# The adaLN half rows of the projection stages are loaded through GpSimd's queue instead of SyncE's, in a hybrid decoder layer on one core

## Chip, core and metric

One NeuronCore of one Trainium2 chip runs the kernel. The metric is the device time of one execution in microseconds (us); the median of three runs before the change is 1996.33 (1995.65 to 1997.18).

The engines are TensorE (PE in the profile, with PEld for its weight loads), VectorE (DVE), ScalarE (ACT), GpSimd (POOL) and SyncE (SP). Each has its own instruction stream, which it works off in order. A transfer between device memory (HBM) and the on-chip memory (SBUF) is issued by an instruction on the stream of one engine, here SP or POOL, and is then moved by the core's 16 DMA engines. An instruction that must wait for a buffer holds up all that stands behind it on its stream, so the stream of SP or POOL is spoken of as a queue.

## What is computed

One decoder layer in float32, for one sequence of 512 tokens and width 2048. A conditioning vector c gives six modulation vectors of 2048 (adaLN):

```
mod = (silu(c) @ w_ada + b_ada).reshape(B, 6, D)        # sh1, sc1, gt1, sh2, sc2, gt2
h = rmsnorm(x, g_mix) * (1 + sc1) + sh1
q, k, v, xr, xg = split(h @ w_in)                       # 5 x 1024 columns
o_attn = stick_breaking_attention(q, k, v)              # 8 heads of 128
xr = causal_depthwise_conv(xr)                          # 4 taps
o_lru = rg_lru(xr) * gelu(xg)
mixed = concat(rmsnorm(o_attn), rmsnorm(o_lru))
x = x + gt1 * (mixed @ w_out)
h = rmsnorm(x, g_mlp) * (1 + sc2) + sh2
x = x + gt2 * (relu(h @ w_mlp_in) ** 2 @ w_mlp_out)
out = rmsnorm(x, g_final)
```

## The kernel before, in words

**Matmuls.** A float32 operand is split into a rounded high part and a low part, and a product is three passes of TensorE (`mm3`, L258 to L263): high x high (L259), weight high x activation low (L262), weight low x activation high (L263). A weight tile comes from HBM into a raw buffer `wr` (`weights`, L236, on SP), ACT copies its high part (L244), VectorE subtracts to get the low part (L245, shown as L122, the helper that records it). There are four `wr` buffers and three each of the high and low parts `wh` and `wl`.

**Modulation rows.** The modulations are not computed on TensorE. Each block of 128 outputs of one modulation is a row block of the transposed `w_ada`: 128 partitions x 2048 values, worked off as two half rows of 128 x 1024 (512 KB). VectorE multiplies each half row by silu(c) (the two tiles `cb`) and sums it in the same instruction (L211); a small step adds the two sums and the bias into `mods` (L220). Six modulations of 16 blocks make 192 half rows. `Rows` (L186 to L222) handles five of the six: `rows` holds SC1 and SH1 (64 half rows, tags EARLY, used from the start of the program to about 195 us), `rows2` holds GT1, SC2 and SH2, in this order (96 half rows). `Rows.load(n, tags)` takes a buffer and issues the next n loads; `Rows.row` makes a modulation's block out of two half rows and loads what is missing. In before all of them are issued on SP.

Until the last X gate group the half rows of `rows2` go with MID: they take buffers "x" only, of which there are four, and are loaded when they are needed, two at a time. From L770 on they go with LATE: buffers "x" and "tt" in turn, five loaded ahead (L771), one more after each half row used.

**Order of the work.** The program is written as a main line of matmul groups with background lanes, generators of small pieces. At each `tick` of the main line a lane may be given pieces, at the lane's pace. A scheduler then places all instructions of each engine by priority; `later()` keeps an instruction at the place at which it was written, relative to the others so marked. Up to about 195 us: the front (norm, conv columns), the first Q and K group. Then `qk_group(2)`, `v_group(4)`, `qk_group(4)`, `qk_group(6)`, `xg_group(0)`, `xg_group(4)`, and the output projection with `w_out` (`product`, L838 to L853), up to about 650 us, with `ensure(GT1)` (L843) ahead of its first evacuation and `ensure(SC2)`, `ensure(SH2)` (L849, L850) near its end. The MLP, some 1340 us, follows.

The lanes beside these groups:

- `pair(h)`: attention of two heads. Scores on TensorE, a causal mask (L635), exponentials on ACT (L637 to L639), sums on VectorE (L641), ACT again (L644), a low part (L645, shown as L122), then cumulative sums as matmuls (L654), and shares (L663 to L666).
- `lru_shift` (L519 to L546): sums the 16 row blocks of the conv columns of `w_in`, each weighted by SH1 (L537), into `accb`. `accb` and the loaded blocks are buffers "x"; `accb` is kept until the 16 matmuls of L542 have read it. Then conv (L551 to L556), gates (L563 to L567, in "x" buffers) and scans (L580).
- `adas(GT1)`, `adas(SC2)`, `adas(SH2)`: the half rows of `rows2`, put into the lane `bg2` ahead of `v_group(4)`.

Evacuations of the groups: Q and K with ACT and VectorE (L459, L460), V with L483 and L484, the output projection with L831 and L362. POOL does two all-reduces over partitions in this part of the program (L336, in the norms of the two mixer halves), and stores the new x to HBM (L1033).

Of the kernel before, what the change touches and what calls it, by code (L numbers as in the profile page):

```python
# [64 lines left out]
def hybrid_layer_kernel(  # L65
# [13 lines left out]
    nc = tc.nc  # L79
# [18 lines left out]
    def T(tag, dt=F32, cols=None):  # L98
        return new(next(split_tag) if tag == "w4" else tag, dt, cols)
# [79 lines left out]
    def later(ins):  # L179
        return tc.keep_in_program_order(ins)  # L180
# [5 lines left out]
    class Rows:  # L186
# [4 lines left out]
            self.tiles = {}  # L191

        def load(self, n, tags):
            queue = nc.sync if tags is MID else nc.sync if tags is LATE else nc.sync
            for _ in range(n):
                if self.todo and tags:
                    i, q = self.todo.pop(0)
                    t = T(next(tags))[:, :1024]
                    later(queue.dma_start(t, w_adaT[i * P : (i + 1) * P, q * 1024 : (q + 1) * 1024]))
                    self.tiles[i, q] = t  # L200
# [24 lines left out]
    MID = itertools.cycle(["x"])  # L225
    LATE = itertools.cycle(["x", "tt"])
# [42 lines left out]
    class Lane:  # L269
# [8 lines left out]
        def next(self):  # L278
            if not self.queue:
                return False  # L280
            try:
                self.wait += next(self.queue[0]) or 0.0
            except StopIteration:
                self.queue.pop(0)
            return True
# [19 lines left out]
    def ending(load, step, ks, done, dt=0.5):  # L305

        w = [load(k) for k in ks]
        for o in range(4):
            for k, w_ in zip(ks, w):
                step(k, w_, [o])  # L310
            done(o)
            tick(dt)
# [94 lines left out]
    EARLY = itertools.cycle(["x", "tt"] * 3 + ["x"])  # L407
# [97 lines left out]
    def v_group(h0):  # L505
        bs = [bank("mm") for _ in range(4)]
        load, step = lambda k: weights(src_v(k, h0, 4)), lambda k, w, os: v_mm(bs, w, k, os)
        for k in range(NK - 2):
            step(k, load(k), range(4))
            tick()  # L510
        ending(load, step, range(NK - 2, NK), lambda o: v_evac(bs, h0, [o]))
# [848 lines left out]
    tags = ["w4"] * 3 + ["w3"] * 2 + ["w4"] * 2 + ["w3"]  # L1360
# [108 lines left out]
```

## Time and profile before

| | before |
|---|---|
| median of 3 runs | 1996.33 us (1995.65 to 1997.18) |
| profiled execution | 1994.49 us, its span 1992.7 |
| granted TensorE clock | 0.996 of full speed, over the whole span |
| busy: TensorE, VectorE, ScalarE, GpSimd | 97%, 88%, 54%, 10% |
| DMA, mean over the span | 223 GB/s; in 230 to 345 us 174, in 520 to 650 us 290 |
| loads of half rows by SP, whole run | 108 into "x" (median landing 5.6 us), 52 into "tt" (6.2 us) |

The span is what the profiler recorded from the first to the last instruction; the execution's own time is 1.8 us longer. The page's busy shares are averages over stages with different limits, so the table of busy time by stretch is read beside them. In the lists of waits a line says which engine stood idle ahead of which instruction, and what ended the wait, as total, number and longest, in us. In a timeline a row is: start, duration, engine, line, operation, what it writes and reads, and in brackets the idle time before it and what ended it. "DMA to landing" is the time from issue to arrival.

### The profile page before, as it was taken

What the parts mean: (1) busy time and instruction counts of PE and PEld (TensorE: products, weight loads), DVE (VectorE), ACT (ScalarE), POOL (GpSimd) and SP (SyncE); (2) the same over time, 40 slices, a digit from 0 to 9 for tenths busy, and PEclk for the clock granted to TensorE, in tenths of its full rate; (3) what the DMA queues carried; (4) which work ended last, traced back from release to release, by engine and by line L of the source; (5) the groups of instructions that cost most, each with busy time, mean ns of one, the idle gap of its engine ahead of it and who ended that gap; (6) DMA issues with size and microseconds to landing.
All of it is one profiled execution on the core that took longest, in us unless ns stands there. A gap on an engine that the chain in (4) does not pass through costs nothing. (4 is left out here: it accounts for less than half of the span.)

```text
span 1992.7 us, 37203 instructions
## 1 busy us (share of the span) xinstructions
PE 1941.9 (97%) x14148; PEld 1815.3 (91%) x14148; DVE 1760.6 (88%) x2979; ACT 1074.6 (54%) x1580; POOL 193.6 (10%) x307
## 2 busy tenths in 40 slices
PE   8999999999999998999999999999999999999997
PEld 6787887788888998999999999999999999999996
DVE  8998776988998599999999999999879779879996
ACT  5443564786433385555555555556445555556552
POOL 0000000000000000112111211200110210211100
PEclk9999999999999999999999999999999999999998
DMA  9896655556779544766666665755567668679653
GB/s 368 304 340 198 212 163 185 179 163 218 226 251 365 170 134 129 239 194 213 221 196 203 226 197 190 232 173 210 185 241 262 238 249 278 220 253 341 225 197 112
DMA packets 205238, 443.51 MB, mean 223 GB/s; under 512 B 20481, under 2 KB 42113, under 8 KB 205058
## 3 DMA queue, kind: packets, MB, share of 16 engines
q1 hardware_dynamic: 176338, 356.58, 54.2%
q0 software_dynamic: 23680, 77.61, 10.5%
q10 hardware_dynamic: 5040, 6.93, 1.0%
q8 instruction: 111, 1.82, 0.4%
q14 instruction: 69, 0.57, 0.1%
HBM read 376.30 MB, written 64.75 MB: 221 GB/s over the span
## 5 line engine op out<-in xcount | busy, mean ns | idle before, releaser
L1102 PE MATMUL ps_mm<-a,w 128*128 128x256 f32 x1696 | 469.1, 277 | 3.0 <-DVE a L1114 1.2
L1104 PE MATMUL ps_mm<-a,w 128*128 128x256 f32 x1696 | 469.2, 277 | 0.4 <-DVE w L122 0.3
L1103 PE MATMUL ps_mm<-a,w 128*128 128x256 f32 x1696 | 469.1, 277 | 0.4 <-DVE a L122 0.3
L1072 ACT ACTIVATE w<-ts 128x1024 fp32r<-128x1024 f32 x244 | 258.4, 1059 | 273.1 <-DVE ts L1068 241.5
L1104 PE MATMUL ps_z<-a,w 128*128 128x256 f32 x1304 | 362.0, 278 | 6.9 <-DVE w L122 6.8
L1102 PE MATMUL ps_z<-a,w 128*128 128x256 f32 x1304 | 362.2, 278 | 3.4 <-DVE a L1118 1.6
L1103 PE MATMUL ps_z<-a,w 128*128 128x256 f32 x1304 | 361.4, 277 | 0.1
L122 DVE TENSOR_TENSOR w<-ts,w 128x1024 fp32r<-128x1024 f32 x244 | 297.8, 1221 | 55.4 <-PE ps_mm L1103 20.4
L1102 PEld LDWEIGHTS ps_mm<-a,w 128*128 128x128 f32 x1696 | 318.4, 188 | 4.3 <-issue 2.5
L1104 PEld LDWEIGHTS ps_mm<-a,w 128*128 128x128 f32 x1696 | 318.7, 188 | 1.1 <-DVE w L122 1.0
L1103 PEld LDWEIGHTS ps_mm<-a,w 128*128 128x128 f32 x1696 | 318.7, 188 | 0.8 <-DVE a L122 0.8
L122 DVE TENSOR_TENSOR w<-raw,w 128x768 fp32r<-128x768 f32 (+1 forms) x296 | 267.5, 905 | 37.8 <-ACT w L244 24.0
L1066 ACT ACTIVATE w<-raw 128x768 fp32r<-128x768 f32 x244 | 204.5, 839 | 174.8 <-issue 80.5
L1104 PEld LDWEIGHTS ps_z<-a,w 128*128 128x128 f32 x1304 | 245.6, 189 | 8.2 <-DVE w L122 8.1
L1102 PEld LDWEIGHTS ps_z<-a,w 128*128 128x128 f32 x1304 | 245.8, 188 | 4.9 <-issue 2.1
L1103 PEld LDWEIGHTS ps_z<-a,w 128*128 128x128 f32 x1304 | 245.7, 188 | 0.6 <-DVE a L122 0.6
L244 ACT ACTIVATE wh<-wr 128x512 fp32r<-128x512 f32 (+1 forms) x184 | 113.2, 618 | 142.4 <-PE ps_mm L262 61.8
L1060 DVE TENSOR_TENSOR ts<-raw 128x512 f32<-128x512 f32 x244 | 166.8, 684 | 14.2 <-DMA raw<-in_w_mlp_out_dram 13.4
L259 PE MATMUL ps_mm<-a,wh 128*128 128x512 f32 x448 | 176.8, 395 | 2.6 <-DVE a L460 1.0
L263 PE MATMUL ps_mm<-a,wl 128*128 128x512 f32 x448 | 175.0, 391 | 1.5 <-DVE wl L122 1.3
L262 PE MATMUL ps_mm<-a,wh 128*128 128x512 f32 x448 | 174.9, 390 | 0.0
L211 DVE SCALAR_TENSOR_TENSOR x<-x,cb 128x1024 f32<-128x1024 f32 x108 | 131.2, 1218 | 23.4 <-DMA x<-in_w_adaT_dram 23.3
(336 smaller groups left out, 4007.7 us busy)
## 6 DMA issues: line engine op xcount, KB each, us to landing
raw<-in_w_mlp_out_dram SPq DMA_DIRECT2D x124, 512.0 KB, 4.6
raw<-in_w_mlp_in_dram SPq DMA_DIRECT2D x120, 512.0 KB, 3.8
x<-in_w_adaT_dram SPq DMA_DIRECT2D x108, 512.0 KB, 5.6
wr<-in_w_in_dram SPq DMA_DIRECT2D x160, 256.0 KB, 3.4
tt<-in_w_adaT_dram SPq DMA_DIRECT2D x52, 512.0 KB, 6.2
part<-a POOLq DMA_DIRECT2D x84, 256.0 KB, 3.9
a<-part SPq DMA_DIRECT2D x84, 256.0 KB, 6.3
prod<-a POOLq DMA_DIRECT2D x63, 256.0 KB, 5.8
```

Of the source, the lines that this page charges most:

```text
L122: tt(out=out, in0=full, in1=f32(high), op=ALU.subtract)
L211: ins = stt(out=t, in0=t, scalar=1.0, in1=cb[q_], op0=ALU.mult, op1=ALU.mult, accum_out=self.ga[:, q_ : q_ + 1],)
L244: act(h[:, :n], r[:, :n], AF.Copy)
L259: first = mm(out, wh, ah, start=start, stop=False, **kw)
L262: mm(out, wh, al, start=False, stop=False, **kw)
L263: mm(out, wl, ah, start=False, stop=stop, **kw)
L1060: tt(out=t[:, : 2 * HT].rearrange("p (a b) -> p a b", a=2), in0=r[:, HT : 3 * HT].rearrange("p (a b) -> p a b", a=2), in1=r[:, q_(0)].unsq ...
L1066: act(h, r[:, HT:], AF.Copy)
L1072: act(h, t, AF.Copy)
L1102: mm(out, wh[:, blk(i)], ah, start=st, stop=False, **kw)
L1103: mm(out, wh[:, blk(i)], al, start=False, stop=False, **kw)
L1104: mm(out, wl[:, blk(i)], ah, start=False, stop=j == js[-1], **kw)
```

## The change

Of the half rows, those of `rows` stay on SP; the 96 of `rows2` are issued by GpSimd:

```
-            queue = nc.sync if tags is MID else nc.sync if tags is LATE else nc.sync
+            queue = nc.sync if tags is EARLY else nc.gpsimd
```

Buffers, tags and arithmetic stay as they are. The number of instructions on TensorE, VectorE and ACT is the same; SP has 96 rows fewer, POOL 96 more. The scheduler places the loads anew, and with them VectorE's multiplications.

SP's queue at about 225 to 250 us, the weights of `qk_group(2)` and `v_group(4)` (wr) and the first half rows of GT1 (x_2448, x_2450, x_2521); - is before alone:

```order
 L236 DMA wr_2319<-in_w_in_dram 128x2x256
 L236 DMA wr_2393<-in_w_in_dram 128x512
-L199 DMA x_2448<-in_w_adaT_dram 128x1024
-L199 DMA x_2450<-in_w_adaT_dram 128x1024
 L236 DMA wr_2455<-in_w_in_dram 128x512
 L236 DMA wr_2477<-in_w_in_dram 128x512
 L236 DMA wr_2498<-in_w_in_dram 128x512
-L199 DMA x_2521<-in_w_adaT_dram 128x1024
```

The half rows are gone from between the weights; they stand on POOL's queue, with nothing else between them there.

VectorE at about 240 to 248 us: wl_2316, wl_2322 and wl_2396 are low parts of weights, tt_2241 a low part of attention scores, ga holds a block's two sums; + is after alone, and the rows with x are half rows of GT1:

```order
 L122 TENSOR_TENSOR tt_2241<-tt_2236,tt_2240 128x1280
 L122 TENSOR_TENSOR wl_2316<-wr_2313,wh_2315 128x512
+L220 SCALAR_TENSOR_TENSOR mods<-ga_2722,vec 128x1
+L211 SCALAR_TENSOR_TENSOR x_2813,ga_2812<-x_2813,cb_81 128x1024
+L211 SCALAR_TENSOR_TENSOR x_2815,ga_2812<-x_2815,cb_82 128x1024
+L122 TENSOR_TENSOR wl_2322<-wr_2319,wh_2321 128x512
 L545 COPY shb<-ps_z_2280 128x16
-L122 TENSOR_TENSOR wl_2322<-wr_2319,wh_2321 128x512
+L220 SCALAR_TENSOR_TENSOR mods<-ga_2812,vec 128x1
+L211 SCALAR_TENSOR_TENSOR x_2916,ga_2915<-x_2916,cb_81 128x1024
+L211 SCALAR_TENSOR_TENSOR x_2918,ga_2915<-x_2918,cb_82 128x1024
+L122 TENSOR_TENSOR wl_2396<-wr_2393,wh_2395 128x512
```

Here the ninth to twelfth half rows of GT1 (x_2813 to x_2918) stand around wl_2322 and ahead of wl_2396; eight more stand further up. Before, two half rows (x_2448 and x_2450) stood ahead of both.

VectorE at about 304 to 315 us, the evacuation of `v_group(4)` (a, out of ps_mm) with half rows of GT1 (x_3000, x_3002, x_3026) between its steps:

```order
 L122 TENSOR_TENSOR wl_2930<-wr_2927,wh_2929 128x512
 L484 TENSOR_TENSOR a_2857<-ps_mm_2389,a_2856 128x256
-L211 SCALAR_TENSOR_TENSOR x_3000,ga_2999<-x_3000,cb_81 128x1024
 L484 TENSOR_TENSOR a_2861<-ps_mm_2389,a_2860 128x256
 L484 TENSOR_TENSOR a_2857<-ps_mm_2390,a_2856 128x256
-L211 SCALAR_TENSOR_TENSOR x_3002,ga_2999<-x_3002,cb_82 128x1024
 L484 TENSOR_TENSOR a_2861<-ps_mm_2390,a_2860 128x256
-L220 SCALAR_TENSOR_TENSOR mods<-ga_2999,vec 128x1
 L362 TENSOR_TENSOR n_1849<-n_1849,tt_2768 128x512
 L484 TENSOR_TENSOR a_2898<-ps_mm_2391,a_2897 128x256
-L211 SCALAR_TENSOR_TENSOR x_3026,ga_3025<-x_3026,cb_81 128x1024
 L122 TENSOR_TENSOR wl_2948<-wr_2945,wh_2947 128x512
```

The three half rows are gone from this place; they stand at about 250 to 275 us of the order before, behind wl_2396.

## Prediction

> **What bounds the kernel now.** First the page's busy shares, then the table of busy time by stretch over the part of the program in which the moved loads run (about 230 to 640 us), then TensorE's waits there, then VectorE's.
>
> ```profile
> PE 1941.9 (97%) x14148; PEld 1815.3 (91%) x14148; DVE 1760.6 (88%) x2979; ACT 1074.6 (54%) x1580; POOL 193.6 (10%) x307
> core 0: us, PE busy (x) PEld busy (x) DVE busy (x) ACT busy (x) POOL busy (x), PEclk, DMA share, GB/s
> 0.00:50.00 50.00, 42.56 (x163) 32.73 (x164) 41.42 (x83) 25.70 (x40) 0.69 (x6) 1.00 0.98 368
> 230.00:345.00 115.00, 113.44 (x544) 94.67 (x543) 80.06 (x142) 63.90 (x101) 0.00 (x0) 1.00 0.54 174
> 520.00:650.00 130.00, 129.54 (x570) 106.63 (x569) 115.36 (x208) 45.70 (x76) 8.80 (x9) 1.00 0.84 290
> ```
>
> TensorE is the bound, at the full granted clock (1.00) in all three stretches, and in the last two, which the change touches, it is busy nearly all the time. An edit that changes no TensorE work can gain only what TensorE waits. These are all of its waits between 165 and 680 us (columns: total us, times, longest):
>
> ```profile
> PE ps_z L654 <- ACT tt L644: 1.8, 2, 1.3
> PE ps_z L259 <- DVE a L484: 1.4, 2, 0.8
> PE ps_mm L263 <- DVE wl L122: 1.3, 1, 1.3
> PE ps_mm L259 <- DVE a L460: 1.0, 2, 0.8
> PE ps_mm L259 <- ACT wh L244: 1.0, 2, 0.5
> PE ps_z L654 <- DVE tt L122: 1.0, 2, 0.8
> PE ps_mm L259 <- DVE mods L220: 0.2, 1, 0.2
> ```
>
> They add up to 7.7 us, 0.39% of 1996.33: no gain can be larger. None of them is a wait for a transfer. The loads reach TensorE only through VectorE, which multiplies each half row (L211) and does all else in program order:
>
> ```profile
> DVE x L211 <- DMA x<-in_w_adaT_dram: 17.1, 8, 4.0
> ```
>
> VectorE waits 17.1 us for half rows between 225 and 340 us. Most of that is cover that it has to spare; what counts is which of VectorE's later results then come after TensorE wants them.
>
> **The change part by part.** The edit removes 96 loads of 512 KB from SP's queue and puts them on POOL's. It changes no arithmetic, but it moves VectorE's order: in the changed program the 22 half rows of GT1 stand earlier. Ten instead of two precede the weight step wl_2322, twelve instead of two precede wl_2396, and x_3000, x_3002 and x_3026 leave the evacuation of the second V group. After about 615 us the order is as before.
>
> *Issue and landing.* The half rows of 230 to 345 us with their landings, the L542 matmuls that read the same kind of buffer, POOL's nearest transfers (256 KB, late in the program), and the page's median for half rows that land in the tt buffers:
>
> ```profile
> L199 SPq DMA_DIRECT2D x<-in_w_adaT_dram x22: 422/426/482, 232.8 to 331.6; - x22
> L211 DVE SCALAR_TENSOR_TENSOR x<-x,cb x22: 1214/1220/1227, 237.8 to 337.0; 128x1024 f32<-128x1024 f32 x22
> L542 PE MATMUL ps_z<-ones,x x16: 167/251/252, 241.8 to 243.4; 128*128 128x2 f32 x16
> DMA to landing us min/median/max: 4.1/5.6/7.5
> ...
> L1255 POOL DMA_DIRECT2D a<-x x20: 546/546/553, 1808.3 to 1921.7; - x20
> DMA to landing us min/median/max: 3.0/4.9/7.1
> ...
> tt<-in_w_adaT_dram SPq DMA_DIRECT2D x52, 512.0 KB, 6.2
> ```
>
> On SP a half row takes 4.1 at least, 5.6 in the middle, from issue to landing. No row shows a 512 KB transfer from POOL's queue. POOL's 256 KB takes 3.0 at least. In the first 50 us the chip moves 368 GB/s with the DMA engines 98% busy, so another 256 KB is 0.7 us more: 3.7 at least. In 230 to 345 us the DMA engines are 54% busy, so weights share them; my estimate is 4.6, with 3.7 and 6.2 (the tt row) as the ends. I take 4.6 since these loads go out one at a time, as buffers come free, while SP's went in pairs, the second behind the first. The Trainium skill, page "DMA: Bandwidth & Descriptors", section "Anatomy of one DMA — SWDGE (gpsimd) path", fits 2.0 us plus the bytes at 436 GB/s for a transfer from this queue, which is 3.2 us here (an estimate); POOL's 256 KB rows, at 3.0 to 7.1, lie above that fit's 2.6, and with 3.2 the sum below would lose its 1.7 and end at -1.1 us. POOL itself is idle there (0.00 in the stretch), and 96 times 0.55 us of issue costs nothing by itself.
>
> *When the early rows run.* VectorE's rows around wl_2322 (243.76) and wl_2396 (247.41), and when TensorE first takes wl_2322's product:
>
> ```profile
> 221.61 2.59 DVE L537 SCALAR_TENSOR_TENSOR x<-x,mods,x 128x1024 f32<-128x1024 f32 x2
> 225.18 1.28 DVE L537 SCALAR_TENSOR_TENSOR x<-x,mods,x 128x1024 f32<-128x1024 f32 x1 [0.23 <-DMA x<-in_w_in_dram]
> 237.77 1.23 DVE L211 SCALAR_TENSOR_TENSOR x<-x,cb 128x1024 f32<-128x1024 f32 x1 [2.88 <-DMA x<-in_w_adaT_dram]
> 243.76 0.68 DVE L122 TENSOR_TENSOR wl<-wr,wh 128x512 fp32r<-128x512 f32 x1
> 247.41 0.69 DVE L122 TENSOR_TENSOR wl<-wr,wh 128x512 fp32r<-128x512 f32 x1
> 253.40 0.69 DVE L460 SCALAR_TENSOR_TENSOR a<-ps_mm,a 128x512 fp32r<-128x512 f32 x1
> ...
> 246.99 0.39 PE L259 MATMUL ps_mm<-a,wh 128*128 128x512 f32 x1
> 247.21 0.39 PE L262 MATMUL ps_mm<-a,wh 128*128 128x512 f32 x1
> 247.44 0.39 PE L263 MATMUL ps_mm<-a,wl 128*128 128x512 f32 x1
> ```
>
> There are four x buffers, but lru_shift's sum (accb) keeps one until its last L542 matmul at 243.4. So the half rows run through three: the first three loads can go when the L537 steps let go of their buffers, at about 222.9, 224.2 and 226.5, and each later load waits for the L211 three half rows before it. The chain to the tenth half row is four landings L, four multiplies (1.2 each) and four hops of about 0.3 (an estimate) from release to issue: 222.9 + 1.5 x 4 + 4L = 228.9 + 4L. Another 0.8 goes to L220 and to other VectorE steps that stand between, and 0.7 to wl_2322 itself: ready at 230.4 + 4L. TensorE wants it at 247.44, so it is late once L is over about 4.3. At 4.6 that is 248.8 by this sum. I replayed VectorE's new order step by step with the same durations, where some hops hide behind other steps: at 4.6 it is 0.8 us late, at 4.4 it is 0.2 late.
>
> The next half rows again stand ahead of what TensorE needs: a_2371 (253.40) and the steps right behind it lose 0.9 more in that replay. The whole loss is 0.0 at L = 4.0, 1.1 at 4.4, 1.7 at 4.6, 2.3 at 4.8, 5.1 at 5.6 and 7.5 at 6.2. I take **+1.7**.
>
> *What goes.* In the second V group three half rows stand among the evacuations (L484), one of them waiting 2.48 us for its landing. TensorE's two rows behind them:
>
> ```profile
> 308.41 1.23 DVE L211 SCALAR_TENSOR_TENSOR x<-x,cb 128x1024 f32<-128x1024 f32 x1 [2.48 <-DMA x<-in_w_adaT_dram]
> ...
> 311.37 0.39 PE L263 MATMUL ps_mm<-a,wl 128*128 128x512 f32 x1
> 311.94 0.47 PE L259 MATMUL ps_mm<-a,wh 128*128 128x512 f32 x1 [0.18 <-DVE mods L220]
> 313.07 0.40 PE L262 MATMUL ps_mm<-a,wh 128*128 128x512 f32 x1
> 314.74 0.50 PE L263 MATMUL ps_mm<-a,wl 128*128 128x512 f32 x1 [1.28 <-DVE wl L122]
> ```
>
> Matmuls of this size start 0.22 to 0.23 us apart when nothing waits (246.99, 247.21, 247.44). The one at 311.94 starts 0.57 after its forerunner, 0.34 too much; the one at 314.74 starts 1.67 after its forerunner, 1.45 too much. The rows have gone from there: **-1.8**. What is late next there is ACT's half of the weights, shown nowhere as later than 0.5.
>
> *A smaller loss.* At 384.51 TensorE already waits for a chain of VectorE's masked sums (L641), ACT (L644) and the cumulative matmuls (L654):
>
> ```profile
> 381.48 1.62 DVE L641 SCALAR_TENSOR_TENSOR tt<-ps_z,tt 128x512 f32<-128x512 f32 x3
> 384.51 0.50 PE L654 MATMUL ps_z<-tt,ntri 128*128 128x512 f32 x1 [1.32 <-ACT tt L644]
> ```
>
> In the changed order the half row x_3518 stands ahead of these L641 instead of behind them. It costs between 0 and its 1.2; I take **+0.7**, past the middle since the chain already ends late.
>
> *What costs nothing.* SP's weight loads no longer stand behind a half row that waits for a buffer, but no TensorE wait names a weight's transfer, and their buffers are what bounds them:
>
> ```profile
> SPq L236 <- DVE wl L122: 254.9, 128, 8.3
> ```
>
> SP's 254.9 us for VectorE's last use of a weight buffer stay. From 520 us on the order of SC2 and SH2 on VectorE is the same, TensorE is 99.6% busy and there is nothing to give back. POOL's queue holds one kind of work that others need: two all-reduces (L336) of the norms, behind which ACT and VectorE wait:
>
> ```profile
> POOL n L336 <- DVE n L362: 450.1, 2, 398.9
> ```
>
> POOL waits 398.9 us for VectorE at one of these and 51.2 at the other. The half rows ahead of them in POOL's queue wait for buffers that come free earlier than the all-reduce's own input, so the issues fall into these waits. Cost 0; uncovered it is one landing, multiply and hop, up to 6.2 + 1.2 + 0.3 = 7.7 us.
>
> **Sum:** 1.7 - 1.8 + 0.7 = +0.6 us. The profiled execution took 1994.49, so it would come to 1995.1; the median of the runs is 1996.33, 1.8 above it, and the forecast stands on that: **1996.9 us**.
>
> **The rivals.**
>
> 1. *The chain of landings dominates* (slower). The same three buffers, with a landing of 5.6 us or more, the middle of SP's rows in this stretch. The loss is 5.1, the sum +4.0, 2000.3; at 6.2 the sum is +6.4, 2002.7; POOL's slowest row, 7.1, would give 11.1 by the same slope (0.4 for each 0.1), and 2006.3. The point from which it decides is L = 5.6. For it: POOL's own 256 KB rows have 4.9 in the middle. Against: those share a nearly full DMA system with other streams. Chance 0.15.
>
> 2. *A descriptor is written only between VectorE's steps* (slower). Then each landing in the chain grows by one VectorE step, 1.2 us, to 5.8: a loss of 5.9 and a sum of +4.8, 2001.1. Against: POOL's 20 issues of L1255 took 546 to 553 ns each beside a busy VectorE, with no long one. Chance 0.06. The Trainium skill, page "SBUF — State Buffer", section "Who interferes with whom", holds that a DMA from the GpSimd queue stalls while VectorE runs copies in its two-port mode; the steps around this chain are mostly two-operand ones, and no run here shows such a stall.
>
> 3. *The half rows ride for free* (faster). L is 4.0 or less, the early rows fit into VectorE's idle time, and the freed order also clears waits for L460, L484 and L654. The V group alone gives -1.8, 1994.5; all waits that stand in the table give -7.7, 1988.6. To be faster by over 0.2% more than half of them (4.0 us) must go, and rows in VectorE's order explain only 1.8. Chance 0.10 for more than 4.0.
>
> 4. *An all-reduce is held up* (slower). A half row ahead of it in POOL's queue waits for a buffer, and the norm comes up to 7.7 us later, 2004.0. It decides once that buffer comes free later than VectorE's last L362. Chance 0.04.
>
> 5. *The queue alone moves nothing*: the landing is the same, VectorE's waits shift and TensorE keeps its 7.7. 1996.3. Against: ten half rows do stand ahead of wl_2322 now. Chance 0.08.
>
> **How the numbers follow.** A measurement of this kernel tells a difference from none at about 0.2%, 4.0 us. The forecast has 0.57 and rival 5 has 0.08, both within 4.0: 0.65. Rivals 1, 2 and 4 make slower: 0.15 + 0.06 + 0.04 = 0.25. Rival 3 makes faster: 0.10. The range reaches down past the V group's -1.8 and half as much again (1993.0) and up to L = 6.2 (2002.7), which leaves out most of rival 3's part, the longest landings and rival 4.
>
> **What would show it.** Right: half rows of POOL that land in 4.4 to 4.8 us between 222 and 245 us, the first issue near 223; VectorE's waits for rows there, before wl_2322; a TensorE wait of about 0.8 us for wl near 247 and another near 254; none at 312 and 315; one near 384 of about 2 us. The stretch from 520 to 650 us unchanged. Wrong: landings above 5.6 or below 4.0, a TensorE wait in any other stretch, an all-reduce that starts later against VectorE's last L362, or waits for L460, L484 and L654 that go away without a row having stood ahead of them.

## The result and the profile after

The changed kernel takes 2002.63 us (median of 16 runs, 1999.77 to 2008.06) against 1996.68 before (16 runs, 1993.36 to 2000.76). The ratio is 1.0030, 95% interval 1.0022 to 1.0038: slower by 6 us, and outside the 0.2% that the prediction took for no change. The profiled execution has a span of 1998.2 us, 5.5 more than before's.

The views are those of before the change: the page's busy shares, then three stretches (of 230 to 345 us its first 30 and last 45, and 520 to 650), then all waits of TensorE between 165 and 680 us:

```profile
PE 1943.5 (97%) x14148; PEld 1818.0 (91%) x14148; DVE 1760.8 (88%) x2979; ACT 1075.2 (54%) x1580; POOL 243.6 (12%) x403
```

```profile
230.00:260.00 30.00, 26.09 (x127) 21.68 (x126) 24.63 (x44) 14.12 (x24) 6.85 (x13) 0.94 0.86 281
300.00:345.00 45.00, 45.00 (x211) 37.59 (x210) 14.99 (x25) 17.98 (x33) 0.00 (x0) 1.00 0.27 80
520.00:650.00 130.00, 127.31 (x559) 104.46 (x558) 117.28 (x210) 47.00 (x78) 28.47 (x47) 1.00 0.83 296
```

```profile
PE ps_mm L263 <- DVE wl L122: 4.3, 3, 2.9
PE ps_z L263 <- DVE wl L122: 2.2, 1, 2.2
PE ps_z L654 <- ACT tt L644: 2.0, 2, 1.4
PE ps_z L259 <- DVE a L484: 1.3, 2, 0.8
PE ps_z L654 <- DVE tt L122: 0.8, 1, 0.8
PE ps_mm L259 <- ACT wh L244: 0.5, 1, 0.5
PE ps_mm L467 <- DVE a L460: 0.2, 1, 0.2
```

POOL issues 96 instructions more and is busy 50 us more; nobody waits for that. TensorE loses nearly 4 us in 230 to 260 us, where the granted clock also falls; it waits for nothing in 300 to 345 us; and it has a new wait of 2.2 us in 520 to 650 us.

A wait list doesn't show what a lower clock costs. So TensorE's matmuls were paired, one by one, between each kernel's trace and before's; the median difference of their start times in a stretch says how far that profiled execution is behind (+) or ahead (-), in us. The stretches are those of before:

| kernel | 220-245 | 262-300 | 322-340 | 390-400 | 550-605 | 620-650 | 1900-end |
|---|---|---|---|---|---|---|---|
| the change | 1.1 | 7.4 | 5.0 | 4.0 | 3.8 | 6.3 | 5.4 |
| e1_mid | 0.9 | 7.2 | 4.8 | 4.0 | 3.7 | 3.7 | 1.9 |
| e2_late | -0.1 | -0.3 | -1.3 | -1.3 | -0.4 | 3.7 | 2.0 |
| e4_pin | 3.9 | 3.7 | 1.3 | 1.9 | 3.7 | 6.4 | 5.0 |
| e5_pinb | 3.8 | 3.5 | 1.2 | 1.7 | 3.6 | 3.6 | 2.4 |
| e11_small | 0.8 | 2.2 | -0.2 | 0.7 | 2.3 | 6.8 | 6.7 |
| e17_smalllate | 0.5 | 5.8 | 3.5 | 2.4 | 5.0 | 8.9 | 3.9 |
| e6_ahead | -0.9 | 6.7 | 4.4 | 3.4 | 3.1 | 7.3 | 9.0 |
| e14a | 1.6 | 1.4 | 3.1 | 2.1 | 1.9 | 1.9 | -1.5 |
| e18_xonly | 2.2 | 9.1 | 6.7 | 7.1 | 6.8 | 14.9 | 16.4 |
| e20a | 0.4 | 0.2 | 5.3 | 4.2 | 4.0 | 4.0 | 6.9 |
| e22_halves | -0.1 | -0.3 | -1.3 | -1.3 | 0.1 | 2.6 | 1.4 |
| e19_actlate | 1.4 | 1.5 | 0.8 | 0.7 | 0.3 | 6.2 | 5.9 |

The first column lies ahead of all that was changed (but for e4_pin and e5_pinb, below): one execution wanders by 1 to 2 us against another there, and as much again in the MLP. Only steps from column to column that repeat in several kernels are read below.

The change loses 6.3 us between 245 and 262, gains 2.4 in the second V group, gains 1.0 near 390, and loses 2.5 near 610: 5.2 in all, with 0.2 of drift between 400 and 605, of a difference of 5.95 in the medians.

**The first loss.** VectorE's row of wl_2316, of the tenth half row, and of wl_2322 in the kernel after; then POOL's first, fourth, seventh and tenth load, which make the chain; then TensorE's two waits, and the granted clock behind them:

```profile
248.22 0.68 DVE L122 TENSOR_TENSOR wl<-wr,wh 128x512 fp32r<-128x512 f32 x1
...
250.96 1.23 DVE L211 SCALAR_TENSOR_TENSOR x<-x,cb 128x1024 f32<-128x1024 f32 x1 [0.78 <-DMA x<-in_w_adaT_dram]
...
252.11 0.69 DVE L122 TENSOR_TENSOR wl<-wr,wh 128x512 fp32r<-128x512 f32 x1
```

```profile
223.91 0.86 POOL L199 DMA_DIRECT2D x<-in_w_adaT_dram  x1 [132.80 <-DMA wr<-in_w_in_dram]
...
231.02 0.53 POOL L199 DMA_DIRECT2D x<-in_w_adaT_dram  x1 [2.93 <-DVE x L211]
...
237.19 0.53 POOL L199 DMA_DIRECT2D x<-in_w_adaT_dram  x1 [1.22 <-DVE x L211]
...
245.45 0.53 POOL L199 DMA_DIRECT2D x<-in_w_adaT_dram  x1 [0.87 <-DVE x L211]
```

```profile
248.96 0.50 PE L263 MATMUL ps_mm<-a,wl 128*128 128x512 f32 x1 [0.97 <-DVE wl L122]
...
252.85 0.50 PE L263 MATMUL ps_mm<-a,wl 128*128 128x512 f32 x1 [2.93 <-DVE wl L122]
...
253.69 0.63 PE L263 MATMUL ps_mm<-a,wl 128*128 128x512 f32 x1
254.12 0.63 PE L259 MATMUL ps_mm<-a,wh 128*128 128x512 f32 x1
```

```profile
252.00:254.00 2.00, 1.15 (x4) 0.98 (x5) 2.00 (x6) 1.08 (x2) 0.53 (x1) 0.90 0.99 348
254.00:256.00 2.00, 2.00 (x6) 1.54 (x6) 1.61 (x5) 2.00 (x5) 0.53 (x1) 0.50 0.99 334
256.00:258.00 2.00, 2.00 (x12) 1.81 (x11) 2.00 (x5) 2.00 (x4) 0.53 (x1) 0.74 1.25 268
```

The four loads landed 5.6, 4.6, 6.6 and 5.5 us after their issue, 5.6 in the mean. TensorE waits 0.97 for wl_2316 and 2.93 for wl_2322. Behind that the clock is at half for some 3.5 us: eight matmuls start 0.43 apart instead of 0.23, 1.6 us more. That is 5.5 of the 6.3; the rest is in starts that are late by less than a view lists. The clock is not a sure part of it: e17_smalllate (below) has the same ten half rows ahead of wl_2322 and a wait of 2.91 us there, keeps the full clock (1.00 in 252 to 258 us), and loses 5.3.

**The second loss.** VectorE evacuates the output projection's first group (L831), for which x is loaded again (xT, L829, 256 KB each, on SP). The loads issued between 585 and 612 us with their landings: before's xT and half rows, then after's xT and half rows (the landings of half rows count those into the tt buffers too); last, TensorE's wait after:

```profile
L829 SPq DMA_DIRECT2D n<-in_xT_dram x3: 377/422/488, 597.9 to 601.2; - x3
...
DMA to landing us min/median/max: 7.2/7.3/8.6
```

```profile
L199 SPq DMA_DIRECT2D x<-in_w_adaT_dram x5: 328/434/710, 584.8 to 605.3; - x5
...
DMA to landing us min/median/max: 5.0/6.6/9.1
```

```profile
L829 SPq DMA_DIRECT2D n<-in_xT_dram x4: 424/428/433, 601.6 to 604.4; - x4
...
DMA to landing us min/median/max: 8.8/10.8/12.6
```

```profile
L199 POOL DMA_DIRECT2D x<-in_w_adaT_dram x6: 527/528/530, 586.7 to 605.4; - x6
...
DMA to landing us min/median/max: 8.5/10.0/10.4
```

```profile
613.61 0.50 PE L263 MATMUL ps_z<-a,wl 128*128 128x512 f32 x1 [2.23 <-DVE wl L122]
```

The first xT tile is issued at the same moment but for the 3.8 us by which all is late; the next two are issued 2.3 to 2.4 us earlier than that. In the trace before, all these loads stand in one queue and land one behind the other: xT at 606.51, a weight at 607.18, xT at 607.84 and 608.50, 0.66 us for each 256 KB. After, a half row of the other queue lands between each two: half row 608.77, xT 610.43, half row 610.68, xT 612.18, half row 613.61, xT 614.08 (and at 611.69 a store of 256 KB that POOL issued). The DMA engines are full in both (0.97 and 1.01 of 600 to 620 us), so SP's queue now gets about a third of them.

VectorE's order has changed here too. These are its rows for the weight step wl_5639 and for the evacuations that wait for xT, first before, then after:

```profile
602.25 0.69 DVE L122 TENSOR_TENSOR wl<-wr,wh 128x512 fp32r<-128x512 f32 x1 [0.89 <-ACT wh L244]
606.53 0.75 DVE L831 SCALAR_TENSOR_TENSOR a<-ps_mm,mods,n 128x512 f32<-128x512 f32 x1 [3.59 <-DMA n<-in_xT_dram]
```

```profile
610.46 0.75 DVE L831 SCALAR_TENSOR_TENSOR a<-ps_mm,mods,n 128x512 f32<-128x512 f32 x1 [5.33 <-DMA n<-in_xT_dram]
612.20 0.75 DVE L831 SCALAR_TENSOR_TENSOR a<-ps_mm,mods,n 128x512 f32<-128x512 f32 x1 [0.99 <-DMA n<-in_xT_dram]
612.87 0.68 DVE L122 TENSOR_TENSOR wl<-wr,wh 128x512 fp32r<-128x512 f32 x1
```

Before, wl_5639 stands ahead of the evacuation that waits 3.59 us for xT, so that wait costs TensorE nothing. After, two evacuations that wait for xT stand ahead of wl_5639, and wl_5639 is what TensorE waits for. The first of the two tiles lands at 610.43, where before's 606.51 and the 3.8 us would put it (610.31).

### The profile page after: what moved, and what is told of

Read it like the earlier page. It is cut to its first block, busy times and chain, and to the rows that moved or that the text cites. A ratio compares the mean times of both kernels' runs of the same rounds, so it can differ in the third digit from the quotient of the medians.

```text
span 1998.2 us, 37293 instructions
## 1 busy us (share of the span) xinstructions
PE 1943.5 (97%) x14148; PEld 1818.0 (91%) x14148; DVE 1760.8 (88%) x2979; ACT 1075.2 (54%) x1580; POOL 243.6 (12%) x403
## 5 line engine op out<-in xcount | busy, mean ns | idle before, releaser
L1060 DVE TENSOR_TENSOR ts<-raw 128x512 f32<-128x512 f32 x244 | 167.0, 685 | 13.4 <-DMA raw<-in_w_mlp_out_dram 12.6
L122 DVE TENSOR_TENSOR wl<-wr,wh 128x512 fp32r<-128x512 f32 (+1 forms) x184 | 124.2, 676 | 47.2 <-ACT wh L244 46.3
```

What stands on the lines that cost most here:

```text
L122: tt(out=out, in0=full, in1=f32(high), op=ALU.subtract)
L1060: tt(out=t[:, : 2 * HT].rearrange("p (a b) -> p a b", a=2), in0=r[:, HT : 3 * HT].rearrange("p (a b) -> p a b", a=2), in1=r[:, q_(0)].unsq ...
```

## The experiments

The theory after the result: two losses in two places with two causes, additive. First, ten half rows ahead of wl_2322 through three buffers, so that four landings follow one another. Second, transfers of a second queue that are not urgent take time from SP's that are. Rivals: the GpSimd queue is slow as such; VectorE's order, not the landings, makes the loss; the second loss only follows the first. Ratios are to the kernel before, with 95% intervals.

### GT1 alone, and the later rows alone

```
 e1_mid:   queue = nc.gpsimd if tags is MID else nc.sync
 e2_late:  queue = nc.gpsimd if tags is LATE else nc.sync
```

> Only GT1's 33 or so half rows of the first kind (MID) go through GpSimd's queue; from the last X gate groups on (LATE) SyncE loads them as before. Two-places theory: the change loses at two independent places, about 5 us where ten half rows stand ahead of wl_2322 (near 247 us), about 2.5 us where the half rows of SC2 and SH2 run ahead on a queue of their own (near 610 us), and gains about 3 in between. So this kernel keeps the first loss and the gain and has no wait of TensorE near 610: about 3.5 us over before (2000.2). Rival, that the first delay makes the second: the wait near 610 stays, about 6 over (2002.6).

> Only the later half rows (LATE) go through GpSimd's queue; the first part of the program is as before. Two-places theory: no TensorE wait over 1 us at 247, the two stalls of the second V group (312 and 315 us) as before, one wait of about 2.2 us for wl near 610: 2.5 us over before (1999.2). Rival, that the wait near 610 only follows from the delay in the first part: same as before (1996.7).

Measured: e1_mid 1998.01 us, 1.0021 (1.0011 to 1.0031); e2_late 1997.71, 1.0014 (1.0004 to 1.0025). In the table e1_mid follows the change up to 605 us and has no step at 610; e2_late follows before up to 605 and has a step of 4.1 at 610, part of it a clock of 0.91 in 600 to 620 us, behind a wait of 2.21. The two losses are independent, and the ratios add up to about the change's.

### The same queue with another order

VectorE's multiplications of GT1 are kept where the program writes them, on POOL's queue (e4_pin) and on SP's (e5_pinb). The edit also holds one multiplication of the front (its tag is None), which costs both kernels 3.3 to 3.7 us in the first 20 us, where no other kernel loses.

```
-                if q is not None:
+                if tags is not EARLY:
                     later(ins)
```

> All 96 half rows through GpSimd's queue as in the change, but VectorE's multiplications of GT1's half rows are kept where the program writes them, so that two instead of ten stand ahead of wl_2322. Order theory: the loss at 247 us is the order's; here no TensorE wait over 1 us there, half-clock stretch gone, only the loss near 610: about 2.5 us over the kernel with the same order on SyncE's queue. Queue theory: transfers on GpSimd's queue are slower as such and TensorE waits for them anyway: 5 us or more over it.

> The kernel before with VectorE's multiplications of GT1's half rows kept where the program writes them, all loads on SyncE's queue: the control for the run with the same order on GpSimd's queue. Both theories: the second V group is freed of its two stalls (1.8 us), nothing is lost elsewhere: 1994.9, between 1993 and 1997.

Measured: e4_pin 2001.79 us, 1.0027 (1.0017 to 1.0037); e5_pinb 1999.04, 1.0021 (1.0011 to 1.0030). e5_pinb was expected faster and was slower, for the front's multiplication and for 2.4 us lost again between 340 and 605. The pair still answers its question: from 220 to 605 us the two stay within 0.2 us of each other. With two half rows ahead of wl_2322, GpSimd's queue costs nothing there:

```profile
L199 POOL DMA_DIRECT2D x<-in_w_adaT_dram x6: 527/528/859, 227.4 to 247.8; - x6
...
DMA to landing us min/median/max: 4.0/5.2/6.1
```

SP's six loads in the twin take 4.3 to 7.4 with 5.5 in the middle. The queue is not slower as such. Near 610 e4_pin loses 2.7 and e5_pinb nothing; wl_5639 stands behind two evacuations in e4_pin and ahead of them in e5_pinb.

### Landing or VectorE's work

GT1's half rows move a quarter of their bytes, with VectorE's time made up.

```
+                    w_ = 256 if tags is MID else 1024
+                    later(queue.dma_start(t[:, :w_], w_adaT[..., q * 1024 : q * 1024 + w_]))
...
+                if tags is MID:
+                    stt(out=t[:, 256:], in0=cb[q_][:, 256:], scalar=1.0, in1=cb[q_][:, 256:], ...)
```

> The changed kernel, where GT1's half rows transfer only their first 256 of 1024 columns; VectorE multiplies these and runs a second step over the other 768 columns of silu(c), so that its busy time is about the same, in about the same order. Left out: three quarters of GT1's sums. Landing theory: VectorE's work alone fits ahead of wl_2322 and the loss near 247 us comes from four landings in a row; here it falls from 5 us or more to under 1, the half-clock stretch goes, and only the loss near 610 is left: about 2 below the kernel before plus 2.5, so 1996 to 1998. Order theory: ten half rows' multiplications ahead of wl_2322 are too many by themselves; the loss near 247 stays over 3 us.

Measured: 2000.51 us, 1.0029 (1.0019 to 1.0040). The time did not fall as expected, but the first loss did. In this kernel's order nine half rows and the longer step of the tenth stand ahead of wl_2322. POOL's loads of 222 to 262 us land in 2.6 to 3.2 us, and TensorE has only these two waits in 230 to 262 us, neither for wl (its line numbers are 4 higher):

```profile
DMA to landing us min/median/max: 2.6/2.7/3.2
```

```profile
256.55 0.50 PE L471 MATMUL ps_mm<-wh,a 128*128 128x512 f32 x1 [0.53 <-ACT wh L248]
257.88 0.51 PE L471 MATMUL ps_mm<-wh,a 128*128 128x512 f32 x1 [0.60 <-DVE a L464]
```

The step there is 1.4 us instead of 6.3. So some 5 us of the first loss are the landings and what hangs on them, 1.4 VectorE's order alone. What this kernel gained there it lost near 385 and at 430 to 450 us (3.2 together) and near 610 (4.5: a wait of 2.55, and the clock at half behind it). The second VectorE step of each half row may be a part of that; it was not told apart.

### Fewer half rows ahead, the later ones on SP

In e14a GT1's second block is kept in place (two half rows ahead of wl_2322), in e20a its third (four).

```
 queue = nc.gpsimd if tags is MID else nc.sync
-                if q is not None:
+                if q is not None or tags is MID and m == GT1 and j in (1,):    # e20a: (2,)
                     later(ins)
```

> GT1's first kind of half rows on GpSimd's queue, the later ones on SyncE's; and GT1's second block alone is kept at the place where the program writes it on VectorE, so that two half rows stand ahead of wl_2322 instead of ten and the rest still run before the second V group. Two-places theory: both losses gone, the gain in the V group (about 2) and near 380 (about 1) kept: 2 to 3 us faster than before, 1993. Rival, that the gain in the V group is only the delay's own slack given back: same as before.

> GT1's first kind of half rows on GpSimd's queue, the later ones on SyncE's, and GT1's third block kept at the place where the program writes it on VectorE: four half rows stand ahead of wl_2322, not ten and not two, so that the last of GT1's do not crowd the stretch near 305 us, where two ahead lost 3.5 us. Two-places theory: no wait over 1 us near 247, under 2 us lost near 305, the gains in the V group (about 2) and near 380 (about 1) kept: the profile's TensorE is 1 to 3 us ahead of before at 450 us, the median 1993 to 1995. Rival, that what is gained at one place of VectorE's order is lost at the next: no time differs from before, 1995 to 1997.

Measured: e14a 1997.51 us, 1.0009 (0.9999 to 1.0018); e20a 1997.09, 1.0004 (0.9992 to 1.0016). Neither beats before; the rival held. The first loss is gone in both (no step at 245 to 262) and so is the second. But the half rows that wait behind wl_2322 now crowd the stretch ahead of the V group, with a wait for another weight there (1.52 us in e14a), in e20a with the clock at 0.81 around it:

```profile
308.29 0.80 PE L469 MATMUL ps_mm<-wl,a 128*128 128x512 f32 x1 [3.87 <-DVE wl L122]
```

```profile
300.00:318.00 18.00, 14.03 (x52) 10.83 (x51) 12.68 (x26) 8.29 (x15) 1.06 (x2) 0.81 0.37 118
```

The profiled execution of e14a, 1992.33 us, was the fastest of its eleven runs; the medians decide.

### The second loss: whose transfers, and how many

e17_smalllate moves a quarter of the later half rows' bytes (the edit of e11_small with LATE in place of MID). e6_ahead loads two ahead, e18_xonly uses four buffers for them.

```
 e6_ahead:   rows2.load(5, LATE)  ->  rows2.load(2, LATE)
 e18_xonly:  LATE = itertools.cycle(["x", "tt"])  ->  itertools.cycle(["x", "x"])
```

> The changed kernel, where the later half rows (from the last X gate groups on) transfer only 256 of 1024 columns, with VectorE's time made up by a second step; GT1's rows are as in the change. Left out: three quarters of the sums of SC2, SH2 and the end of GT1. Shared-transfer theory: the xT tiles land late near 610 us since the half rows on their own queue take transfer time from them; here the TensorE wait for wl near 610 is gone and the loss near 247 stays: 3.5 us over before. Order theory: VectorE's two evacuations ahead of wl_5639 make the loss; the wait stays at 2 us: 6 over.

> The changed kernel with two later half rows loaded ahead instead of five; all bytes are moved. Run-ahead theory: with two transfers outstanding on GpSimd's queue instead of five, the xT tiles land as in before and the TensorE wait near 610 us is gone: 2.5 us less than the change. Rival, that the total of the bytes decides: landings of xT stay at 9 us or more and the wait of about 2 us stays. A third way: the half rows themselves come late and VectorE waits for them.

> The changed kernel in which the later half rows use the four x buffers only, not x and tt in turn. VectorE's order near 610 us is the same as in the change, all bytes are moved. Run-ahead theory: free buffers alone limit how far GpSimd's queue runs ahead; with four buffers instead of eight fewer than five half rows are under way at 600 us, they land in 7 us or less instead of 10, the xT tiles in 8 or less instead of 9 to 13, and the TensorE wait of 2.2 us for wl near 610 shrinks to under 1. Rival, that the order of VectorE's evacuations decides: the wait stays at 2 us or more. A third way: with four buffers VectorE waits for half rows from 520 us on and TensorE loses more than before.

Measured: e17_smalllate 2003.93 us, 1.0042 (1.0027 to 1.0056); e6_ahead 2002.03, 1.0036 (1.0023 to 1.0049); e18_xonly 2006.35, 1.0047 (1.0032 to 1.0061).

With a quarter of the bytes the xT tiles land in 4.5 to 5.5 us, and the wait shrinks from 2.23 to 0.49 (landings of xT, then of half rows, then VectorE's rows around the weight step, then TensorE's row; line numbers are 4 higher):

```profile
DMA to landing us min/median/max: 4.5/4.7/5.5
...
DMA to landing us min/median/max: 2.6/2.9/4.0
```

```profile
612.26 0.75 DVE L835 SCALAR_TENSOR_TENSOR a<-ps_mm,mods,n 128x512 f32<-128x512 f32 x1 [1.11 <-DMA n<-in_xT_dram]
612.93 0.68 DVE L122 TENSOR_TENSOR wl<-wr,wh 128x512 fp32r<-128x512 f32 x1
613.53 0.74 DVE L835 SCALAR_TENSOR_TENSOR a<-ps_mm,mods,n 128x512 f32<-128x512 f32 x1
```

```profile
613.67 0.50 PE L267 MATMUL ps_z<-a,wl 128*128 128x512 f32 x1 [0.49 <-DVE wl L122]
```

This does not show that the shared transfers make the loss, for the order moved as well: one evacuation stands ahead of the weight step here, two in the change. The order alone would give the same wait. In the change the first evacuation is over at 611.13 (610.46 and 0.67); a weight step begun then would let TensorE start 0.74 us later, at 611.87, and it was ready at 611.38: 0.49 late (an estimate from those rows). The other way round, with the change's order and the second xT tile landing 0.66 us behind the first, as before, the weight step would begin at 611.80 and TensorE would be 1.2 us late instead of 2.2 (an estimate likewise). So the order makes at least half of this wait, and the slower landings add at most 1.1 us. Over the kernels (e19_actlate, with another order, is told below) the wait goes with the order:

| kernel | evacuations ahead of wl_5639 (of its counterpart, where the numbers differ) that wait for xT | TensorE's wait for it |
|---|---|---|
| before, e1_mid, e5_pinb, e14a, e20a | none | none |
| e17_smalllate | one | 0.49 |
| the change, e2_late, e4_pin, e11_small, e6_ahead, e22_halves | two | 2.21 to 2.55 |
| e18_xonly | two | 4.44 |

No run moved these transfers to POOL's queue and kept VectorE's order, or the other way round, so how the 2.5 us divide stays open.

e17_smalllate as a whole was slower than expected: it loses 3.9 us between 605 and 650, more than the change, in small steps that go on from 500 to 630 us. VectorE has its second steps to do there; whether they are the cause was not tested.

e6_ahead did not do what it was to do: the half rows of 590 to 605 us are issued at the same places and land in 10 us as in the change. POOL's loads go out as buffers come free, so the count loaded ahead binds nothing here. e18_xonly did limit the buffers: the half rows land in 4.8 to 8.5 us. The xT tiles still take 10 to 11.6, and VectorE now also waits for half rows:

```profile
DVE a L831 <- DMA n<-in_xT_dram: 7.8, 2, 6.6
DVE x L211 <- DMA x<-in_w_adaT_dram: 3.6, 7, 0.9
```

The run-ahead theory falls: with four buffers instead of eight the xT tiles land no sooner. With two evacuations still ahead of wl_5639, VectorE's wait of 6.6 us for xT goes on into TensorE's, which is 4.44.

### What the share hangs on

e22_halves splits each later half row into two transfers of 2 KB a partition; e19_actlate puts them on ScalarE's queue.

```
 e22_halves:   for s_, n_ in ((0, 512), (512, 512)): queue.dma_start(t[:, s_ : s_ + n_], ...)    # LATE, gpsimd
 e19_actlate:  queue = nc.scalar if tags is LATE else nc.sync
```

> Only the later half rows go through GpSimd's queue, each as two transfers of 512 columns (2 KB a partition, as the xT tiles on SyncE's queue have) instead of one of 1024 (4 KB). Turn theory: the 16 DMA engines are full near 600 us and take turns between the two queues piece by piece, so that a half row's 4 KB pieces get twice the bytes of xT's 2 KB pieces; in the run with whole half rows the xT tiles land one by one, 1.8 us apart, with a half row between each two. With pieces of the same size they land about 1.3 us apart, in 7 to 10 us from issue, and the TensorE wait of 2.2 us near 610 shrinks to 1 or less. Rival, that the share does not hang on the pieces: landings of 9 to 12.6 and a wait of 2.2 as there.

> Only the later half rows go through another queue, ScalarE's, not GpSimd's; VectorE's order near 600 us differs a little, since the half rows come earlier. Second-queue theory: any queue beside SyncE's shares the DMA engines in the same way, half rows there land in 9 us or more where the engines are full, and xT's landings stretch to 9 us or more. GpSimd theory: it is GpSimd's queue that is slow, and from ScalarE's the half rows land in 5 to 7 us as on SyncE's. ScalarE's own work stands behind its loads when they wait for a buffer, so the time may be longer for that alone: 1997 to 2005.

Measured: e22_halves 1998.61 us, 1.0013 (0.9996 to 1.0030); e19_actlate 2001.82, 1.0024 (1.0008 to 1.0040). Smaller pieces change nothing (a wait of 2.2 us, xT as slow as e2_late's 5.7 to 12.6; landings of xT, first line e22_halves, second e19_actlate):

```profile
DMA to landing us min/median/max: 5.8/8.8/13.2
```

```profile
DMA to landing us min/median/max: 7.2/7.6/7.9
```

From ScalarE's queue xT lands as in before, two of the tiles 0.65 us apart, and the half rows in 5.9 to 8.9. That speaks for GpSimd's queue taking the larger share, but these loads were issued at other moments, xT 6 to 8 us later, so the two aren't quite alike. Its order differs too (wl_5639 stands ahead of both evacuations), and it loses some 6 us between 605 and 650 all the same: TensorE waits 1.89 us for the weight step behind the two evacuations, and ScalarE's own work stands behind its loads, which was not taken apart. The Trainium skill, page "DMA: Bandwidth & Descriptors", section "Queues, rings and completion order", has each DMA engine take turns between queues, a whole packet at a time; the turns agree with the half rows and xT tiles that land alternately, and the some two thirds for POOL's queue do not follow from the size of the pieces, as e22_halves shows. What sets the share stays open.

## Why the prediction was right or wrong

The time fell into the range, at its upper end (2002.63 of 2002.7); the likeliest case, no change (+0.6), did not come, and the prediction gave 0.15 to the mechanism that made the larger loss. That the time still lies inside is in part luck: 2.5 us came from a place that was priced at 0, and two other terms came out lower than forecast and made up for some of it. By the steps:

- **Landing, 4.6 us: wrong in size.** The chain's four landings were 5.6 in the mean, the median of the 17 loads of 222 to 262 us 5.4. The argument that loads which go out one at a time land sooner failed: bringing 22 half rows forward fills the DMA engines (0.86 of 230 to 260 us, where before had 0.50). The bound of 6.2 and rival 1's point of 5.6 held it.
- **The chain of three buffers and its price: right.** Rival 1 gave 5.1 us at L = 5.6; waits and what follows came to 6.3. The term left out is the clock: behind the wait of 2.93 us TensorE ran at half for some 3.5, 1.6 us more (e17_smalllate, where the clock stayed full, lost 5.3). e11_small shows the landings in it, e4_pin that it isn't the queue.
- **The V group, -1.8: right** in place and sign. The starts gain 2.3 to 2.4 between 308 and 322 us in all kernels in which the half rows leave it, but also 0.7 to 1.0 in e2_late, e22_halves and e19_actlate, where they stay. So about 1.4 is theirs.
- **x_3518, +0.7: too large.** TensorE's wait for L644 at that place is 1.40 instead of 1.32. The table's fall of 1.0 between 340 and 400 is another matter: about half of it lies near 366, where before's wait of 0.77 for L460 is gone and one of 0.43 for wl has come. What took the L460 wait away was not traced.
- **"What costs nothing": wrong, 2.5 us.** The prediction looked at SP's weights, which bound nothing, and took VectorE's order from 520 us on from the half rows of SC2 and SH2 alone. It missed that wl_5639 moves from ahead of the evacuations to behind two of them. And it didn't look at the third kind of load on SP there, xT, whose landing VectorE already waited 3.6 us for before the change. It noted that the DMA engines are busy in 520 to 650 us (0.84) and drew nothing from it. How much of the 2.5 is the order and how much the slower landing stays open.
- **The all-reduce and the stalled descriptors (rivals 4 and 2): not seen.** POOL's issues in the stretch of the chain took 0.53 us, the first 0.86, beside a VectorE that is busy 24.63 of 30 us, and no wait of TensorE names what follows the all-reduces. The chain's 5.6 is near rival 2's 5.8 too, but SP's loads, which POOL does not issue, took 5.5 in the middle in e5_pinb.

The sum by its stretches, predicted and measured: first loss +1.7 and +6.3; V group -1.8 and -2.4; 340 to 400 us +0.7 and -1.0; near 610 us 0 and +2.5. The lower end of the range, 1993.0, is 0.6 below what its own words give (1996.33 less 1.8 and half as much again is 1993.6); nothing hangs on it.

## What to carry to other kernels

A load that moves to another queue moves its consumer in a scheduler's order too: read what now stands ahead of each result that the bound engine waits for, and count the landings in a row that the free buffers allow, at the landing time of the fuller stretch that this itself makes. Compare the order of everything else on that engine as well, not of the moved work alone: here a weight step slid behind two evacuations that wait for a transfer, and a wait that had cost nothing reached the bound engine. One queue is also an order of urgency. Where the DMA engines are full, a queue of their own for the transfers that can wait slowed the ones that somebody waits for; look for such a transfer, even off the critical path.

## What the hardware showed

- Two queues share full DMA engines in turns: on SP's queue 256 KB loads landed 0.66 us apart with nothing of POOL's between them, and 1.8 to 1.9 apart beside half rows on POOL's. With POOL's pieces cut from 4 KB to 2 KB a partition, xT landed as late (e22_halves 5.8 to 13.2 us, e2_late 5.7 to 12.6).
- Between 227 and 260 us a 512 KB load took about as long from POOL's queue (e4_pin, 4.0 to 6.1 us) as from SP's (e5_pinb, 4.3 to 7.4).
- The granted clock fell to half for about 3.4 us behind waits of TensorE of 2.93 us (the change, at 253), 2.21 (e2_late, near 610), 2.04 (e1_mid, at 251) and 1.52 (e14a, at 308), and for about 6.8 us around the wait of 3.87 (e20a). It stayed full behind 2.91 (e17_smalllate, at 251) and behind 2.23 and 2.35 near 610 (the change, e4_pin), so the length of a single wait doesn't decide it. The Trainium skill, page "TensorE: Matmul & The Clock Gate", section "HAM oscillation — how this bites in real kernels", puts the limit at idle gaps over about 3.4 us; here waits of 1.5 to 2.9 were enough in some cases.
